# Modulation products of a diffusion layer queued on VectorE behind weight splits, and redistributed over the stages

## The chip, the cores and the metric

The kernel runs on one core of a Trainium2 chip. The metric is device time in microseconds, the median of three runs. Besides the three timed runs there is one execution with the hardware profiler, from which all rows below come.

## The reference, cut to what matters

One layer of a diffusion backbone in f32: 256 latent tokens and 256 context tokens, model width D = 2048, feed-forward width 5632. Six rows of modulation, each 2048 long, are computed from the condition vector and scale, shift and gate the two sub-layers:

```python
sh_m, sc_m, gt_m, sh_f, sc_f, gt_f = split(silu(c) @ w_ada + b_ada, 6)
h_lat = x * (1 + sc_m) + sh_m                 # the same for the context tokens
...                                           # h @ w_in: q, k, v, gates, decay; linear attention, pooling
mix = (gate_gla * y_gla + gate_pool * y_pool) @ w_out
x = layer_norm(ALPHA * x + gt_m * mix)
ffn = (silu(h2 @ w_gate) * (h2 @ w_up)) @ w_ffn_out      # h2 = x * (1 + sc_f) + sh_f
x = layer_norm(ALPHA * x + gt_f * ffn)
```

The first two rows of modulation (shift and scale of the mixer) are needed before anything else. The change is about how the other four, gt_m, sh_f, sc_f and gt_f, are computed: 4 x 2048 dot products of length 2048, done beside the rest of the layer.

## The kernel before

**Weights.** Every matrix arrives in units of 128 x 1024 f32 (512 KB). `weights` (L102) takes a unit: `raw_unit` issues its load on SP's queue (L95) into a ring of three buffers `raw`; `split` rounds it to a high part `hi` on ScalarE (L99) and forms the rest, `lo = raw - hi`, on VectorE (L100); TensorE multiplies both, `hi` with 512 columns (L128) and `lo` with 256 (L132) for stages where the weights stand still, or in three products (L158, L159, L161) where they move. A `raw` buffer is free, and the load of the unit three further on can be issued, when VectorE's subtraction has read it.

**Modulation products.** `ada(n)` (L252) does the next n units of 96: it loads 128 rows of the transposed modulation matrix on the same SP queue (L264, `w_adaT`) into a buffer `ra`, and VectorE multiplies them with the condition row and adds up each row (L265, a product with accumulator read; the result goes to one column of `mods`). `ra` is a ring too: of `NAK` = 3 buffers during keys and q, of one during gates and heads, of `NRA` = 2 during the merge. A load waits on SP for the product that last used its buffer, and everything behind it on SP waits with it.

`ada` is called at places that the tuple `ADA` counts: after each of the 16 key tiles (`ADA[2]` units), after each q tile (`ADA[1]`), after each gate block behind the first (`ADA[5]`), and after each column tile `ct` of the merge (`ADA[3]`, and all that is left from `ct` = 13 on). Entries 0 and 4 are for the values at the start, where no buffer for products exists yet. The last 32 units, gt_f, are done within the FFN, tiles 12 to 39, one a tile and two in every eighth (L874 to L876), in a ring of three inside the buffer `fa`.

**Order.** The program says what depends on what. A scheduler with a priority heap gives each engine its order; the splits of weights have raised priority (`high_priority(PW)`). `tc.issue_after(ins)` adds an edge: the instruction may stand in its engine's order only behind `ins`. Before, the products have no such edge, and the scheduler may place them as soon as their buffer and load allow.

**Stages** in the trace of before: values up to 239 us, keys to 335, first half of q to 358, gates, heads and pooling to 614, merge (16 column tiles of 7 weight units) to 944, the output projection w_o to 1048, the FFN's first matrices (44 tiles of 4 units, w_fi) to 1553, its last matrix to 1801. `rows(i)` (L749) loads the layer norm's gain and bias on POOL's queue, twice 1 MB; `rows(1)` takes the place of `fa` after the last product of the FFN. `add_mods` sums the finished columns, and `bcast_cols` (L727) spreads gt over the partitions for the residual (L755).

## Time and profile before

| | us |
|---|---|
| timed runs: lowest, median, highest | 1811.80, 1814.71, 1817.25 |
| profiled execution, its own time | 1810.72 |
| its span in the trace | 1808.9 |
| TensorE busy (PE) | 1754.6 |
| VectorE busy (DVE) | 1163.7 |
| ScalarE busy (ACT) | 804.3 |
| mean granted TensorE clock | 0.991 of full speed |

The profiled execution is 4.0 us faster than the median; 1.8 us of it lie outside the span. In rows of the trace each line gives a start and a duration in us, the engine, the line in the code, the operation and its tiles (`ps<-h,hi` reads "ps written from h and hi"), how many instructions the row joins (x8), and in brackets for how long the engine had been idle before it and what released it. PE's matmuls are pipelined, so that rows overlap a little. Windows show for each engine the busy time within the window.

### The profile page before, as it was taken

Reading aid. Unit: us, or ns where it says so; the run is one execution under the profiler, and the core shown is the slowest. Engines: PE = TensorE matmul, PEld = TensorE weight load, DVE = VectorE, ACT = ScalarE, POOL = GpSimd, SP = SyncE. Lnnn points to the kernel's source line nnn. Section 1 sums busy time; section 2 is a strip of 40 time slices with the busy share of each in tenths; the row PEclk is TensorE's granted clock in tenths of the full one; section 3 lists DMA queues with packets and bytes.
Section 4 is the critical chain, followed back from the end, with each engine's and each line's share of the span. In section 5 each row is a group of like instructions: output and inputs, shape, how many; then the busy total and the mean of one; then the engine's idle time right before and its main releaser. Section 6 shows DMA issues by size and latency. Waiting matters only on the chain.

```text
span 1808.9 us, 24699 instructions
## 1 busy us (share of the span) xinstructions
PE 1754.6 (97%) x9520; PEld 1469.2 (81%) x9520; DVE 1163.7 (64%) x1729; ACT 804.3 (44%) x1181; POOL 9.1 (1%) x19
## 2 busy tenths in 40 slices
PE   6999999999999999999999989999999999999996
PEld 4667888877777788888887878888878888888886
DVE  2555486587778788765556756677855556554555
ACT  2122222374776444454444454454444444433332
POOL 0000000000000000000000000000000000000000
PEclk9999999999999999999999989999999999999998
DMA  9796276666335798865566535579865555555553
GB/s 351 261 360 225 97 263 210 236 223 215 123 107 187 240 311 306 275 205 188 187 245 223 196 126 189 186 280 314 313 243 188 187 189 183 187 197 191 193 188 127
DMA packets 109637, 394.14 MB, mean 218 GB/s; under 512 B 12208, under 2 KB 12848, under 8 KB 109008
## 3 DMA queue, kind: packets, MB, share of 16 engines
q1 hardware_dynamic: 107712, 384.06, 62.3%
q0 software_dynamic: 1808, 8.52, 1.3%
q8 instruction: 74, 1.21, 0.3%
q14 instruction: 43, 0.35, 0.1%
HBM read 390.43 MB, written 2.10 MB: 217 GB/s over the span
## 4 chain that ended last, share of the span: by engine, by line
PE 80%; DMA 10%; DVE 6%; issue 2%; ACT 2%; SPq 0%; DVEq 0%; ACTq 0%
PE ps L128 28%; PE ps L132 14%; PE ps L158 11%; PE ps L159 10%; PE ps L161 10%; DMA ra<-in_w_adaT 5%; DVE lo L100 2%; PE ps L279 2%; DMA fa<-in_w_adaT 1%; DMA raw<-in_w_o 1%; ACT hi L99 1%; PE ps L504 1%; PE ps L547 1%; DMA raw<-in_w_fi 1%; DVE ra L265 1%
## 5 line engine op out<-in xcount | busy, mean ns | idle before, releaser
L100 DVE TENSOR_TENSOR lo<-raw,hi 128x1024 fp32r<-128x1024 f32 x510 | 622.2, 1223 | 391.5 <-ACT hi L99 384.1
L99 ACT ACTIVATE hi<-raw 128x1024 fp32r<-128x1024 f32 x510 | 539.0, 1059 | 643.0 <-PE ps L159 214.3
L128 PE MATMUL ps<-h,hi 128*128 128x512 f32 x1408 | 357.5, 396 | 4.5 <-ACT hi L99 3.7
L128 PEld LDWEIGHTS ps<-h,hi 128*128 128x128 f32 x1408 | 255.9, 191 | 51.4 <-ACT hi L99 4.1
L128 PE MATMUL ps<-hl,hi 128*128 128x512 f32 x768 | 211.1, 392 | 0.5 <-ACT hi L99 0.5
L132 PEld LDWEIGHTS ps<-h,lo 128*128 128x128 f32 x1408 | 193.1, 191 | 15.9 <-DVE lo L100 2.2
L132 PE MATMUL ps<-h,lo 128*128 128x256 f32 x1408 | 198.1, 283 | 0.4 <-DVE lo L100 0.4
L265 DVE SCALAR_TENSOR_TENSOR ra<-ra,silb 128x1024 f32<-128x1024 f32 x96 | 117.2, 1222 | 72.3 <-DMA ra<-in_w_adaT 71.6
L128 PEld LDWEIGHTS ps<-hl,hi 128*128 128x128 f32 x768 | 139.3, 189 | 25.9 <-ACT hi L99 0.7
L158 PE MATMUL ps<-hi,hl 128*128 128x512 f32 x320 | 128.9, 404 | 9.1 <-ACT hi L99 7.9
L158 PE MATMUL ps<-hi,hid 128*128 128x512 f32 (+1 forms) x372 | 134.9, 369 | 0.0
L159 PE MATMUL ps<-hi,hid 128*128 128x512 f32 (+1 forms) x372 | 134.0, 369 | 0.0
L159 PE MATMUL ps<-hi,hl 128*128 128x512 f32 x320 | 126.2, 396 | 0.0
L132 PE MATMUL ps<-hl,lo 128*128 128x256 f32 x768 | 120.5, 282 | 0.0
L132 PEld LDWEIGHTS ps<-hl,lo 128*128 128x128 f32 x768 | 111.7, 190 | 7.0 <-DVE lo L100 0.2
L161 PE MATMUL ps<-lo,hl 128*128 128x512 f32 x320 | 93.2, 392 | 0.0
L161 PE MATMUL ps<-lo,hid 128*128 128x512 f32 x372 | 90.6, 369 | 0.0
L330 DVE TENSOR_TENSOR v<-ps,v 128x512 f32<-128x512 f32 x80 | 50.6, 683 | 59.3 <-PE ps L161 59.3
L158 PEld LDWEIGHTS ps<-hi,hl 128*128 128x128 f32 x320 | 60.4, 189 | 28.4 <-ACT hi L99 8.7
L158 PEld LDWEIGHTS ps<-hi,hid 128*128 128x128 f32 x372 | 69.9, 188 | 12.2 <-DVE xt L759 0.2
L159 PEld LDWEIGHTS ps<-hi,hid 128*128 128x128 f32 x372 | 70.0, 188 | 11.9
L161 PEld LDWEIGHTS ps<-lo,hid 128*128 128x128 f32 x372 | 66.2, 188 | 11.8
(248 smaller groups left out, 2087.2 us busy)
## 6 DMA issues: line engine op xcount, KB each, us to landing
raw<-in_w_fi SPq DMA_DIRECT2D x176, 512.0 KB, 3.8
ra<-in_w_adaT SPq DMA_DIRECT2D x96, 512.0 KB, 4.6
raw<-in_w_fo SPq DMA_DIRECT2D x88, 512.0 KB, 4.3
rw<-in_w_sh_sc SPq DMA_DIRECT2D x64, 512.0 KB, 8.0
raw<-in_w_bg SPq DMA_DIRECT2D x64, 512.0 KB, 4.3
raw<-in_w_v SPq DMA_DIRECT2D x32, 512.0 KB, 5.6
raw<-in_w_g SPq DMA_DIRECT2D x32, 512.0 KB, 4.3
raw<-in_w_go SPq DMA_DIRECT2D x32, 512.0 KB, 4.3
```

Of the source, the lines that this page charges most:

```text
L99: S.activation(hi, full, AF.Copy)
L100: return V.tensor_tensor(lo, full, hi.bitcast(F32), op=ALU.subtract)
L128: PE.matmul(o, hi[:, j * P:(j + 1) * P], act(n + j), start=(n + j == 0), stop=(n + j == nk - 1), skip_group_check=True)
L132: PE.matmul(o[:, :T], lo[:, j * P:(j + 1) * P], act(n + j)[:, :T], start=False, stop=(n + j == nk - 1), skip_group_check=True)
L158: PE.matmul(o, ah, hi[:, a:b], start=(n + j == k0), stop=False)
L159: PE.matmul(o, al, hi[:, a:b], start=False, stop=False)
L161: PE.matmul(o, ah, lo[:, a:b], start=False, stop=(n + j == end))
L265: V.scalar_tensor_tensor(r, r, 1.0, silb[half], op0=ALU.mult, op1=ALU.mult, accum_out=mods[:, half, i:i + 1])
L279: PE.matmul(pr[32 * g:32 * g + 32, :256], sil[:, kt, :], r[:, 256 * g:256 * g + 256], start=(u == 0), stop=(u == KT // per - 1), skip_grou ...
L330: V.tensor_tensor(dst, src, dst, op=ALU.add)
L504: PE.matmul(ex[:, :n], la[:, s, t, c * P:(c + 1) * P], cw[:, :n], start=(s == 0), stop=(s == 1))
L547: PE.matmul(scc[:, t * T:(t + 1) * T], kst[:, c, t * P:(t + 1) * P], q4[:, c].rearrange("p t i -> p (t i)"), start=(c == 0 and t == 0), st ...
```

## The change

`ADA` becomes (0, 1, 4, 2, 8, 8): four products instead of two behind each key tile, eight instead of twelve behind each gate block, and the rest of the 96 in the merge is taken from `ct` = 14 on, not 13. Every product gets an edge behind a split: those of `ada` behind the split that was written last in the program (`last_split`), those of the FFN behind the split of `hid`, the tile's result (`lo_ins`). Loads have no edge of their own. The number of products and loads stays as it was. Line numbers after the change are one to four higher.

```diff
--- before.py
+++ after.py
@@ -38,7 +38,7 @@
 PRI = 300
 GROUPS = {0: 2, 2: 2, 4: 2, 6: 2, 8: 4, 12: 4}
 STEPS = {0: 2, 2: 3, 4: 4, 6: 4, 8: 2, 12: 0}
-ADA = (0, 1, 2, 2, 8, 12)
+ADA = (0, 1, 4, 2, 8, 8)
 
 
 S_CT = 0
@@ -81,6 +81,7 @@
         return tc.tile_pool(name=name, bufs=1, space=bass.MemoryType.PSUM, reuse_waits="tile")
 
     cnt = [0]
+    last_split = []
 
     def nm(s):
         cnt[0] += 1
@@ -97,7 +98,8 @@
 
     def split(full, hi, lo):
         S.activation(hi, full, AF.Copy)
-        return V.tensor_tensor(lo, full, hi.bitcast(F32), op=ALU.subtract)
+        last_split[:] = [V.tensor_tensor(lo, full, hi.bitcast(F32), op=ALU.subtract)]
+        return last_split[0]
 
     def weights(src):
         r = raw_unit(src)
@@ -262,8 +264,9 @@
                     silu_row(silb[half], half)
                 r = pool.tile([P, U], F32, tag="ra", bufs=ada_bufs[-1], name=nm("ra"))
                 nc.sync.dma_start(r, w_adaT[64 * half + i])
-                V.scalar_tensor_tensor(r, r, 1.0, silb[half], op0=ALU.mult, op1=ALU.mult,
-                                       accum_out=mods[:, half, i:i + 1])
+                with tc.issue_after(last_split[0].ins):
+                    V.scalar_tensor_tensor(r, r, 1.0, silb[half], op0=ALU.mult, op1=ALU.mult,
+                                           accum_out=mods[:, half, i:i + 1])
 
 
         def ada_chunk(ci):
@@ -705,7 +708,7 @@
             V.tensor_tensor(sg, sg, sp, op=ALU.add)
             m = mT[ct // 8][:, ct % 8]
             split(sg, m[:, 0, :], m[:, 1, :])
-            ada(ADA[3] if ct < 13 else 128)
+            ada(ADA[3] if ct < 14 else 128)
 
 
         add_mods(0, 3)
@@ -873,8 +876,9 @@
                 half, i = divmod(fu, 16)
                 r = fa[:, fu % 3, :]
                 nc.sync.dma_start(r, w_adaT[64 * half + 48 + i])
-                V.scalar_tensor_tensor(r, r, 1.0, silf[half], op0=ALU.mult, op1=ALU.mult,
-                                       accum_out=mods[:, half, 48 + i:49 + i])
+                with tc.issue_after(lo_ins.ins):
+                    V.scalar_tensor_tensor(r, r, 1.0, silf[half], op0=ALU.mult, op1=ALU.mult,
+                                           accum_out=mods[:, half, 48 + i:49 + i])
                 fu += 1
         if f == 41:
             add_mods(3, 4)
```

What the edges and counts move is seen in the order of the engines. First SP in the FFN, where the products begin: `raw<-in_w_fi` is a load of a weight unit, `fa<-in_w_adaT` one of a product. Before:

```order
L875 DMA fa<-in_w_adaT 128x1024 x2
L95 DMA raw_10246<-in_w_fi 128x1024
L875 DMA fa<-in_w_adaT 128x1024
L95 DMA raw_10276<-in_w_fi 128x1024
L95 DMA raw_10298<-in_w_fi 128x1024
L95 DMA raw_10325<-in_w_fi 128x1024
L875 DMA fa<-in_w_adaT 128x1024
L95 DMA raw_10347<-in_w_fi 128x1024
L875 DMA fa<-in_w_adaT 128x1024
L95 DMA raw_10377<-in_w_fi 128x1024
L875 DMA fa<-in_w_adaT 128x1024
```

and with the change:

```order
L878 DMA fa<-in_w_adaT 128x1024 x2
L96 DMA raw_10246<-in_w_fi 128x1024
L878 DMA fa<-in_w_adaT 128x1024
L96 DMA raw_10276<-in_w_fi 128x1024
L96 DMA raw_10298<-in_w_fi 128x1024
L96 DMA raw_10325<-in_w_fi 128x1024
L878 DMA fa<-in_w_adaT 128x1024 x2
L96 DMA raw_10347<-in_w_fi 128x1024
L96 DMA raw_10377<-in_w_fi 128x1024
L96 DMA raw_10399<-in_w_fi 128x1024
L96 DMA raw_10426<-in_w_fi 128x1024
L878 DMA fa<-in_w_adaT 128x1024
```

Before, product loads alternate with weight loads, so that all 32 go out among 41 weight loads; with the change one follows four weight loads (two in tiles 12, 20, 28 and 36), through tile 39.

The second place is VectorE in the merge, from the split of one column tile's result (`mT`) on. `ra,mods<-ra,silb` is a product, `lo<-raw,hi` the split of a weight unit, `yt` and `ys` are the tile's sums. Before:

```order
L100 TENSOR_TENSOR mT_5018<-yt_5332,mT_5018 128x256
L141 TENSOR_TENSOR yt_5513<-ps_5468,yt_5513 128x256
L265 SCALAR_TENSOR_TENSOR ra_6729,mods<-ra_6729,silb_4576 128x1024
L100 TENSOR_TENSOR lo_5592<-raw_5589,hi_5591 128x1024
L265 SCALAR_TENSOR_TENSOR ra_6732,mods<-ra_6732,silb_4576 128x1024
L100 TENSOR_TENSOR lo_5618<-raw_5615,hi_5617 128x1024
L141 TENSOR_TENSOR yt_5513<-ps_5518,yt_5513 128x256
L265 SCALAR_TENSOR_TENSOR ra_6910,mods<-ra_6910,silb_4576 128x1024
L100 TENSOR_TENSOR lo_5653<-raw_5650,hi_5652 128x1024
L100 TENSOR_TENSOR lo_5675<-raw_5672,hi_5674 128x1024
L141 TENSOR_TENSOR ys_5514<-ps_5566,ys_5514 128x256
L265 SCALAR_TENSOR_TENSOR ra_6913,mods<-ra_6913,silb_4576 128x1024
L701 TENSOR_TENSOR yt_5513<-ys_5514,yt_5513 128x256
```

and with the change:

```order
L101 TENSOR_TENSOR mT_5030<-yt_5344,mT_5030 128x256
L268 SCALAR_TENSOR_TENSOR ra_5474,mods<-ra_5474,silb_4183 128x1024
L268 SCALAR_TENSOR_TENSOR ra_5477,mods<-ra_5477,silb_4183 128x1024
L101 TENSOR_TENSOR lo_5582<-raw_5579,hi_5581 128x1024
L143 TENSOR_TENSOR yt_5525<-ps_5480,yt_5525 128x256
L101 TENSOR_TENSOR lo_5604<-raw_5601,hi_5603 128x1024
L101 TENSOR_TENSOR lo_5630<-raw_5627,hi_5629 128x1024
L143 TENSOR_TENSOR yt_5525<-ps_5530,yt_5525 128x256
L101 TENSOR_TENSOR lo_5665<-raw_5662,hi_5664 128x1024
L101 TENSOR_TENSOR lo_5687<-raw_5684,hi_5686 128x1024
L143 TENSOR_TENSOR ys_5526<-ps_5578,ys_5526 128x256
L704 TENSOR_TENSOR yt_5525<-ys_5526,yt_5525 128x256
```

Before, products lie between most splits, four to five a column tile, and are used up after some seven tiles; with the change two lie together behind the split of `mT`, in every tile up to the last but one.

The third place is VectorE between the first half of q and the first gate weights. The last split of a q weight is `lo_2743` before and `lo_2791` with the change, the first gate weight's is `lo_2970` and `lo_3018`. Before:

```order
L100 TENSOR_TENSOR lo_2721<-raw_2718,hi_2720 128x1024
L142 SCALAR_TENSOR_TENSOR qT<-ps_2617,qT 128x256
L265 SCALAR_TENSOR_TENSOR ra_3748,mods<-ra_3748,silb_1935 128x1024
L100 TENSOR_TENSOR lo_2743<-raw_2740,hi_2742 128x1024
L142 SCALAR_TENSOR_TENSOR qT<-ps_2667,qT 128x256
L265 SCALAR_TENSOR_TENSOR ra_3751,mods<-ra_3751,silb_1935 128x1024
L100 TENSOR_TENSOR lo_2970<-raw_2967,hi_2969 128x1024
L100 TENSOR_TENSOR lo_2988<-raw_2985,hi_2987 128x1024
L100 TENSOR_TENSOR lo_3006<-raw_3003,hi_3005 128x1024
```

and with the change:

```order
L101 TENSOR_TENSOR lo_2741<-raw_2738,hi_2740 128x1024
L268 SCALAR_TENSOR_TENSOR ra_2762,mods<-ra_2762,silb_1935 128x1024
L101 TENSOR_TENSOR lo_2769<-raw_2766,hi_2768 128x1024
L144 SCALAR_TENSOR_TENSOR qT<-ps_2665,qT 128x256
L101 TENSOR_TENSOR lo_2791<-raw_2788,hi_2790 128x1024
L268 SCALAR_TENSOR_TENSOR ra_2812,mods<-ra_2812,silb_1935 128x1024
L556 MEMSET PT_2833 128x256
L556 MEMSET PT_3378 128x256
L144 SCALAR_TENSOR_TENSOR qT<-ps_2715,qT 128x256
L101 TENSOR_TENSOR lo_3018<-raw_3015,hi_3017 128x1024
L473 SCALAR_TENSOR_TENSOR wd_2830<-wd_2830,sm,wr_2828 64x512
L101 TENSOR_TENSOR lo_3036<-raw_3033,hi_3035 128x1024
```

Before, a product stands directly ahead of the last q split and another ahead of the first gate split; with the change another weight's split lies between the product and the last q split, and the product behind it is the last one before the gate splits.

## Rows read from the trace of the kernel before

**Rows 1.** The page's first part: busy time of each engine, share of the span, instructions.

```profile
PE 1754.6 (97%) x9520; PEld 1469.2 (81%) x9520; DVE 1163.7 (64%) x1729; ACT 804.3 (44%) x1181; POOL 9.1 (1%) x19
```

**Rows 2.** The page's groups of instructions: the split on VectorE and the products; after the bar busy us and mean ns of one, then idle time ahead of them.

```profile
L100 DVE TENSOR_TENSOR lo<-raw,hi 128x1024 fp32r<-128x1024 f32 x510 | 622.2, 1223 | 391.5 <-ACT hi L99 384.1
...
L265 DVE SCALAR_TENSOR_TENSOR ra<-ra,silb 128x1024 f32<-128x1024 f32 x96 | 117.2, 1222 | 72.3 <-DMA ra<-in_w_adaT 71.6
```

**Rows 3.** The page's DMA issues: the loads for the products, with the median us from issue to landing.

```profile
ra<-in_w_adaT SPq DMA_DIRECT2D x96, 512.0 KB, 4.6
```

**Rows 4.** TensorE's timeline, FFN behind the last product: starts of two units, 16 units apart.

```profile
1346.64 2.00 PE L128 MATMUL ps<-h,hi 128*128 128x512 f32 x8
...
1391.34 2.00 PE L128 MATMUL ps<-h,hi 128*128 128x512 f32 x8
```

**Rows 5.** TensorE's timeline, FFN with the last products: the start of a unit, the longest wait and the half unit behind it, and the start of the unit 14 further on than the first.

```profile
1290.71 1.55 PE L128 MATMUL ps<-h,hi 128*128 128x512 f32 x6
...
1329.78 3.78 PE L128 MATMUL ps<-h,hi 128*128 128x512 f32 x8 [2.87 <-ACT hi L99]
1333.35 1.91 PE L132 MATMUL ps<-h,lo 128*128 128x256 f32 x8
...
1338.27 2.00 PE L128 MATMUL ps<-h,hi 128*128 128x512 f32 x8
```

**Rows 6.** Windows in the FFN: window, its us, busy us (x instructions) of PE, PEld, DVE, ACT and POOL, granted clock, DMA share, GB/s.

```profile
1250.00:1300.00 50.00, 50.00 (x288) 43.78 (x287) 40.01 (x59) 23.18 (x34) 0.00 (x0) 1.00 0.87 310
...
1320.00:1330.00 10.00, 7.13 (x42) 6.15 (x42) 3.70 (x9) 3.50 (x7) 0.18 (x1) 0.96 0.94 365
1330.00:1340.00 10.00, 10.00 (x40) 8.50 (x41) 7.27 (x10) 5.38 (x8) 0.00 (x0) 0.70 0.63 210
...
1350.00:1400.00 50.00, 50.00 (x289) 44.02 (x288) 28.68 (x37) 24.01 (x37) 0.00 (x0) 1.00 0.59 188
```

**Rows 7.** The chain of work that ended last, from 1270 to 1330 us: start, duration, what. Only its transfers are copied.

```profile
1274.96 4.92 DMA fa<-in_w_adaT
...
1307.39 7.32 DMA fa<-in_w_adaT
...
1320.08 8.48 DMA raw<-in_w_fi
```

**Rows 8.** POOL's timeline: the two issues of `rows`.

```profile
936.21 1.05 POOL L752 DMA_DIRECT2D rows<-in_lnrows  x2 [340.85 <-PE ps L132]
...
1319.13 1.05 POOL L752 DMA_DIRECT2D rows<-in_lnrows  x2 [127.67 <-DVE sg L856]
```

**Rows 9.** TensorE's timeline in the merge: the start of a unit, two waits, and the start of the unit 18 further on than the first.

```profile
694.92 2.00 PE L128 MATMUL ps<-hl,hi 128*128 128x512 f32 x8
...
706.04 1.21 PE L132 MATMUL ps<-y,lo 128*128 128x256 f32 x8 [0.36 <-DVE lo L100]
707.77 0.96 PE L128 MATMUL ps<-hl,hi 128*128 128x512 f32 x3 [0.52 <-ACT hi L99]
...
748.60 1.78 PE L128 MATMUL ps<-hl,hi 128*128 128x512 f32 x7
```

**Rows 10.** Windows in the keys, the end of the pooling stage, the merge, and the end of the merge with the start of w_o; columns as in rows 6.

```profile
240.00:270.00 30.00, 30.00 (x164) 26.08 (x163) 26.01 (x44) 5.11 (x8) 0.61 (x1) 1.00 0.91 313
...
600.00:640.00 40.00, 39.11 (x211) 33.88 (x212) 31.86 (x50) 20.98 (x34) 0.00 (x0) 1.00 0.80 264
...
660.00:680.00 20.00, 20.00 (x116) 17.58 (x115) 16.34 (x24) 9.19 (x14) 0.00 (x0) 1.00 0.94 328
...
900.00:950.00 50.00, 50.00 (x281) 43.73 (x280) 28.67 (x38) 22.80 (x33) 1.05 (x2) 1.00 0.69 242
```

**Rows 11.** Timelines of VectorE, SP's queue, ScalarE and TensorE between q and the gates.

```profile
347.48 1.23 DVE L100 TENSOR_TENSOR lo<-raw,hi 128x1024 fp32r<-128x1024 f32 x1 [0.57 <-ACT hi L99]
...
350.83 1.23 DVE L265 SCALAR_TENSOR_TENSOR ra<-ra,silb 128x1024 f32<-128x1024 f32 x1 [1.80 <-DMA ra<-in_w_adaT]
...
353.06 1.28 SPq L95 DMA_DIRECT2D raw<-in_w_g  x3
...
359.34 1.06 ACT L99 ACTIVATE hi<-raw 128x1024 fp32r<-128x1024 f32 x1 [5.41 <-DMA raw<-in_w_g]
...
360.45 0.50 PE L158 MATMUL ps<-hi,hl 128*128 128x512 f32 x1 [2.19 <-ACT hi L99]
...
368.12 0.39 PE L490 MATMUL ps<-cm,la 128*128 128x256 f32 x1 [2.14 <-ACT la L99]
```

**Rows 12.** Timelines of VectorE and TensorE at the end of the last head.

```profile
597.52 1.23 DVE L265 SCALAR_TENSOR_TENSOR ra<-ra,silb 128x1024 f32<-128x1024 f32 x1 [2.24 <-DMA ra<-in_w_adaT]
...
600.36 0.66 PE L590 MATMUL ps<-sm,o 128*128 128x128 f32 x4 [1.43 <-DVE o L588]
```

**Rows 13.** Timelines of VectorE and TensorE in the FFN without products: a split of a weight, and the matmuls that read it.

```profile
1511.84 1.23 DVE L100 TENSOR_TENSOR lo<-raw,hi 128x1024 fp32r<-128x1024 f32 x1 [1.23 <-ACT hi L99]
...
1518.88 1.11 PE L132 MATMUL ps<-h,lo 128*128 128x256 f32 x8
```

**Rows 14.** VectorE's timeline: the first product of the broadcast of gt_m.

```profile
954.22 0.68 DVE L736 TENSOR_TENSOR dg<-sm,fs 128x512 fp32r<-128x512 f32 x1
```

**Rows 15.** TensorE's timeline in the keys: starts of two units that follow each other.

```profile
296.54 0.40 PE L128 MATMUL ps<-hl,hi 128*128 128x512 f32 x1
...
302.11 0.40 PE L128 MATMUL ps<-hl,hi 128*128 128x512 f32 x1
```

## The prediction

> **What bounds the kernel now.** I read the share of each engine first, then the table of windows of 10 to 50 us, then the timelines of the windows in which TensorE was not busy throughout. TensorE is busy for 97% of the span [rows 1], so a gain can only come from stretches in which it stood still or ran at less than its full clock. In the change's territory there are four such stretches; the first step is to price each.
>
> The product that is moved costs VectorE 1222 ns, about as much as the split's second half, 1223 ns [rows 2], and it brings one 512 KB load that lands in about 4.6 us [rows 3]. A weight unit has the same size. So what the products do to TensorE is read as load on the DMA engines and as place in VectorE's queue.
>
> *FFN.* Where nothing disturbs it, unit follows unit in (1391.34 - 1346.64) / 16 = 2.794 us [rows 4]. Between the starts at 1290.71 and 1338.27 lie 14 units; they took 47.56 us and not 14 x 2.794 = 39.1, which is a **loss of 8.45 us** [rows 5]. It is one wait of 2.87 us for a weight's first half at 1329.78 with smaller ones before it, and then a stretch at half the pace: 3.57 us from one half unit to the next at 1333.35, where 1.84 is usual, the granted clock 0.70 in that window [rows 5, 6]. A mean of 0.70 says that the lower of the two levels (1.2 GHz) was granted for part of it; the engine had just been idle. What released that wait is a chain of loads, each waiting for a product and each product for its load, 4.9 to 7.3 us a link, with a weight's load of 8.48 us at its end [rows 7]. By the listing, all 32 product loads go out among 41 weight loads: 73 x 0.524 MB in 41 x 2.794 = 114.6 us would need 334 GB/s, while the window before the stall moves 310 (and one after the products 188) [rows 6]. At 310 the 73 loads take 123.5 us, 8.9 more, which is about the loss: for these ten tiles the kernel is bound by its loads, and the buffers put off the bill until 1329. At 1319.13, with the last product just over, the POOL queue sends two 1 MB rows into the same engines [rows 8].
>
> *Merge.* The same mechanism, weaker: 18 units from 694.92 to 748.60 took 53.68 us against 50.29, a **loss of 3.4 us**, in small waits as at 706.04 and 707.77 [rows 9], while the window before ran at 328 GB/s [rows 10].
>
> *From q to the gates.* VectorE's product at 350.83 waits 1.80 us for its own load; the second half of the last q weight stands behind it and ends at 353.2, about when SP may issue the first gate load (353.06), which reaches ScalarE at 359.34; TensorE stood **2.19 us** at 360.45 and 2.14 at 368.12 [rows 11].
>
> *Heads.* At 597.52 a product holds up the normalisation for 2.24 us of waiting, and TensorE loses **1.43 us** at 600.36 [rows 12].
>
> **The change part by part.** Nothing is added: 96 and 32 products, the same bytes. The edge behind the split is only an order on VectorE's own queue, so it costs no instruction; I take 0 for it.
>
> 1. *FFN products behind hid's split.* SP now has one product load for four weight loads in most tiles: 5 loads per 4 x 2.794 = 11.2 us, an estimate of 235 GB/s, up to 282 in the four tiles that have two, against 310 before the stall [rows 6]. No link of the chain of loads then follows directly on another, since each product lies a tile behind the last and its ring of three was refilled long ago. I take back the whole 8.45 us. Lower bound: the clock and the waits stay because the POOL rows still come, gain 0 (rival A). On VectorE the product fits into the idle time: it stood 1.23 us before the split at 1511.84, where no product lies [rows 13]. If it is late by a whole product (1.3 us with its accumulator read), the cover is the lead of that split: it ends at 1513.07 and its matmuls start at 1518.88, 5.8 us later [rows 13]. Two products in a row (2.6 us) stay under it too.
>
> 2. *Merge, two products per column tile.* 9 loads in 7 units, 9 x 0.524 MB / 19.6 us = 241 GB/s (estimate), where the four to five products a tile of before made it 295 to 321. Both follow the mT split, 2.6 us against the 5.8 of cover. Gain 3.4; bounds 0 and 3.4. The products now last into column tile 14, some 30 us before the end of this stage at about 944. Their sums go through the small modulation steps into the broadcast, whose first product before was at 954.22 [rows 14]; so about 40 us are left and I cost it at nothing. Without that cover, the w_o residual would wait for them.
>
> 3. *Keys, four products per tile.* Two weight loads and four product loads per tile. A key unit takes 302.11 - 296.54 = 5.57 us [rows 15], so 6 x 0.524 MB / 11.14 us = 282 GB/s (estimate). The trace has 313 GB/s in the first 30 us of the keys with TensorE busy for 30.00 of 30.00 us [rows 10]. Three products in a row are 3.9 us, behind a split of 1.2: 5.1 of 5.57 us. Cost 0; upper bound in rival B.
>
> 4. *q to the gates.* No product stands directly ahead of the last q split now, so the 1.80 us of waiting and the product's own 1.2 leave the path to the first gate load. One unit of 2.79 us behind the split before it (347.48), it would start at 350.3 and not, behind the product, at 352.0: 1.7 us earlier [rows 4, 11]; the first gate load then goes out alone and not as one of three, and 6.3 us of landing should come nearer to the 4.6 of a usual one [rows 3, 11]. Together that is more than TensorE's wait of 2.19, so it goes: gain 2.2. Bounds: 0, if what holds the load is the two loads of constants whose buffers the gate weights take, and 4.3, if the second wait goes too.
>
> 5. *Gates and heads.* 28 products with a ring of one. The wait at 597.52 may go (gain 1.4), but the listing puts products between other steps of a normalisation, each good for 1.3 us if it lands there without waiting. I set 0, with bounds +3 and -3: two such waits either way, by the nearest row, 1.43 [rows 12].
>
> Sum: -8.5 - 3.4 - 2.2 = -14.1 us. I round to 13.5, since the POOL rows, moved to a later place, may take a little there. On the profiled execution (1810.72 us, of which 1808.9 are span) that gives 1797.2. The median of the three runs is 1814.71, 4.0 above the profiled one; against it the forecast is **1801 us**. A difference of 0.3% (5.4 us) is about what a measurement of this kernel can tell from none.
>
> **The rivals.**
>
> *A. The FFN stall only moves.* rows(1) takes the buffer of the product loads, so its two 1 MB transfers follow the last product, then near 1319, now near the end of the FFN's tile 39. If they alone starve the weights, the 8.48 us load comes back there [rows 7]. For it: the stall sits exactly behind the issue at 1319.13 [rows 8]. Against it: the first rows(0) pair, issued at 936.21, met the w_o weights and eight x loads, and its window 900 to 950 has TensorE busy for 50.00 of 50.00 us [rows 8, 10]; and small waits precede 1319 already, with weights' buffers empty from the products. It would leave 8.45 us in place: 14.1 - 8.45 = 5.6 less than before, 1809.1. The page "DMA: Bandwidth & Descriptors" of the Trainium skill, section "Queues, rings and completion order", has each DMA engine take turns between the queues it serves, a packet at a time; by that rule the POOL rows would take about half of the engines as long as they last, wherever they are issued. The trace agrees only so far: the weight's load doubles at 1320.08 but nothing stalls after 936.21 [rows 6, 7, 10].
>
> *B. The keys become bound by their loads.* The rate needed is 282 GB/s; the stretch 600 to 640, also split between a ring of products and weights, moved only 264 [rows 10]. At 264 a tile takes 6 x 0.524 / 264 = 11.9 us, 0.8 more, over eight tiles 6 us. Time 1801 + 6 = 1807. Against it: 313 in the keys themselves.
>
> *C. Slower: products hold the path in gates and heads.* With a ring of one, a load starts only after the product before it, and lands 4.6 us later [rows 3]. Where two products lie close together, on either side of a decay step or a normalisation that TensorE waits for, the second holds that step up to 4.6 us. Before, such a wait of 2.24 us cost TensorE 1.43 at the one place shown [rows 12]. It decides from three such places on: 3 x 4.6 = 13.8 us eats the gains of the other parts. Priced at one in four of the 28 products that the listing leaves to q's second half and the heads, 7 x 4.6 = 32 us, the time is 1801 + 32 = 1833. For it: VectorE takes its queue in order, and a split behind such a product waits too. Against it: VectorE is busy for 64% only [rows 1], and the program places 12 products fewer there (24 after the gate blocks, not 36).
>
> *D. It does not do what it says on the chip.* SP and VectorE take their queues in order, but a product that had to wait before may still be the one that waits: the loads bunch again behind the x, row and gate loads, and the stalls return at other places, with no change, 1811 to 1817. Against it: the listing has the loads one by one among the weights.
>
> **How the numbers follow.** My forecast, gains in FFN and merge without a new loss: 0.58. A: 0.14. B: 0.08. C: 0.10. D: 0.10. Faster by over 0.3% (under 1809.3) takes in the forecast, B, and two thirds of A's cases, which lie about 1809 where the whole stall comes back and lower where part of it does: 0.58 + 0.08 + 0.09 = 0.75. Within 0.3%: the rest of A, D and a little of C, 0.05 + 0.10 + 0.02 = 0.17. Slower: 0.08. For the range the best case is 1814.7 - 8.45 - 3.4 - 4.3 - 3 = 1795.6, with the 2 us that medians of three differ by 1793.5; at the upper end it reaches over A, B and a part of D to 1813. That leaves out C (0.10), the upper part of D and the little below.
>
> **What the profile of the changed kernel would show.** Step 1: the FFN's windows all with 288 or 289 matmuls in 50 us and a clock of 1.00, no wait of ScalarE over 2 us for w_fi, and product loads at even distances. Step 2: no wait of TensorE in the merge windows, with about 240 GB/s up to the last column tiles. Step 3: still no gap in the keys, at some 280 GB/s. Step 4: no wait at the first gate matmul. Step 5: waits of VectorE for w_adaT smaller in sum. The prediction is wrong if a stall of several us follows the POOL rows near the end of the FFN (A), if TensorE waits in the keys (B), or if the gates show more TensorE waits behind a product (C).

## The result and the profile after

The changed kernel takes 1800.24 us, the median of six runs, against 1813.32 for the kernel before beside it: a ratio of 0.9934, 95% interval 0.9917 to 0.9951, or 13.1 us. The forecast was 1801 us. Its profiled execution takes 1799.62 us with a span of 1797.8, which is 11.1 us shorter than the span of before.

Where those 11.1 us lie is read from TensorE's timeline: a stage lasts from the first matmul of its kind to the first of the next. The same table serves the experiments below (us; "gates to merge" holds gates, heads, pooling and merge, which overlap).

| execution | values | keys, first half of q | gates to merge | w_o | FFN, first matrices |
|---|---|---|---|---|---|
| before | 221.86 | 121.23 | 583.68 | 104.34 | 504.42 |
| changed | 222.12 | 119.05 | 584.53 | 104.29 | 494.96 |
| e1_ffn_edge | 222.93 | 122.34 | 584.90 | 108.66 | 494.89 |
| e2_ada_edge | 224.96 | 119.50 | 611.86 | 109.21 | 505.29 |
| e3_counts | 222.80 | 128.30 | 582.93 | 104.91 | 506.21 |
| e4_no_ffn_edge | 222.98 | 119.15 | 584.01 | 106.96 | 506.70 |
| e5_rows_late | 225.93 | 121.62 | 583.35 | 106.83 | 504.81 |
| e12_rows_wait | 223.06 | 121.94 | 587.85 | 106.63 | 501.47 |
| e6_cross_late | 222.90 | 119.02 | 594.23 | 113.35 | 494.83 |
| e7_one_row | 223.42 | 119.01 | 578.52 | 107.19 | 496.79 |
| e8_after_again | 223.40 | 119.03 | 584.12 | 108.91 | 495.47 |
| e9_own_tmp | 224.86 | 119.35 | 582.75 | 107.13 | 495.23 |
| e10_own_tmp_late | 221.98 | 119.49 | 585.08 | 106.63 | 495.57 |
| e11_heads_free | 223.40 | 119.35 | 582.94 | 106.94 | 495.33 |

So the FFN gives 9.46 us and the edge to the gates 2.18; from gates to merge, where 3.4 were expected, 0.85 is lost; the rest, with 0.54 at the very start, is noise. The w_o stage, in code that no kernel here touches, varies from 104 to 109 us between executions (113.35 in e6, whose last products reach into it): smaller differences than that are read from a stage, not from a total.

Two of these columns join several things. In the FFN, what the change aimed at lies between the first matmul of tile 13 and that of tile 25 (tiles counted from 0). First before, where tile 25 starts at 1338.27 [rows 5], with a window at the start of the FFN, then changed:

```profile
1195.74 1.09 PE L128 MATMUL ps<-h,hi 128*128 128x512 f32 x4
...
1048.00:1053.00 5.00, 4.53 (x13) 3.66 (x14) 2.39 (x6) 2.46 (x7) 0.00 (x0) 0.54 0.00 0
```

```profile
1192.24 1.09 PE L130 MATMUL ps<-h,hi 128*128 128x512 f32 x4
...
1326.32 0.86 PE L130 MATMUL ps<-h,hi 128*128 128x512 f32 x3
...
365.18 0.39 PE L493 MATMUL ps<-cm,la 128*128 128x256 f32 x1 [0.45 <-ACT la L100]
```

These twelve tiles took 142.53 us and take 134.08 now, 8.45 less. The first tile of the FFN is 1.84 us shorter, which the change did not do: TensorE waits 5.11 us at the end of w_o in both kernels, and before, the lower clock behind that wait reached into the FFN (0.54 in its first 5 us, 1.00 in the changed kernel). The last three tiles take 0.82 us more, 36.68 against 35.86; they take 0.7 to 1.3 more in every execution with the FFN's edges.

From gates to merge, the second wait of rows 11, 2.14 us at 368.12, is down to 0.45 (the last row above), which gives 1.7; the last 1728 matmuls ahead of w_o take 301.68 us and not 305.11, which gives 3.4. As the column lost 0.85 all the same, 6.0 us were lost in between, in the heads. The three executions of the changed kernel's code up to there (changed, e8 and e4) lie within 0.5 us of each other, the four of the old code (before, e1, e5 and e12) between 583.35 and 587.85.

The windows of the changed kernel in the keys, the merge, the FFN where the stall was [rows 6], and its last tiles (columns as in rows 6):

```profile
240.00:335.00 95.00, 95.00 (x540) 83.59 (x538) 62.54 (x97) 24.03 (x34) 0.72 (x1) 1.00 0.76 263
...
640.00:760.00 120.00, 120.00 (x689) 105.60 (x688) 85.27 (x120) 58.82 (x88) 0.00 (x0) 1.00 0.71 239
1300.00:1350.00 50.00, 50.00 (x288) 44.04 (x287) 32.27 (x44) 24.28 (x36) 0.00 (x0) 1.00 0.73 239
1500.00:1550.00 50.00, 49.27 (x268) 42.36 (x267) 31.36 (x44) 25.75 (x39) 1.05 (x2) 1.00 0.61 219
```

and the merge window of before:

```profile
640.00:760.00 120.00, 118.24 (x670) 102.55 (x669) 100.56 (x158) 55.65 (x82) 0.00 (x0) 1.00 0.88 303
```

TensorE is busy throughout in the keys, the merge and the FFN's window at full clock; only near the FFN's end is a little missing. In the merge it runs 689 matmuls instead of 670 in 120 us, at 239 GB/s instead of 303; 19 matmuls at 0.174 us are 3.3 us, as the 3.4 above. The products themselves, on the page, beside the lines of rows 1 and 2:

```profile
PE 1751.0 (97%) x9520; PEld 1469.6 (82%) x9520; DVE 1165.7 (65%) x1729; ACT 802.4 (45%) x1181; POOL 9.1 (1%) x19
...
L268 DVE SCALAR_TENSOR_TENSOR ra<-ra,silb 128x1024 f32<-128x1024 f32 x96 | 114.9, 1221 | 9.8 <-DMA ra<-in_w_adaT 9.5
```

They cost as much as before (1221 ns), but VectorE's idle time ahead of them fell from 72.3 to 9.8 us. Between q and the gates (answering to rows 11: SP's queue, ScalarE, TensorE):

```profile
350.80 0.33 SPq L96 DMA_DIRECT2D raw<-in_w_g  x1
...
357.01 1.06 ACT L100 ACTIVATE hi<-raw 128x1024 fp32r<-128x1024 f32 x1 [0.94 <-DMA raw<-in_w_g]
...
357.99 0.40 PE L160 MATMUL ps<-hi,hl 128*128 128x512 f32 x1
```

The first gate load leaves 2.3 us earlier, reaches ScalarE as long after its issue as before (6.2 us), and TensorE does not wait. In the heads there is a wait that no row of before has. ScalarE, SP's queue, POOL and TensorE:

```profile
482.60 0.58 POOL L194 DMA_DIRECT2D silb<-in_c_row  x1 [13.50 <-DVE ra L268]
...
482.75 13.69 SPq L96 DMA_DIRECT2D raw<-in_w_g  x3
...
488.46 1.06 ACT L180 ACTIVATE raw<-silb 128x1024 f32<-128x1024 f32 x1 [4.28 <-DMA silb<-in_c_row]
489.43 0.58 ACT L508 ACTIVATE bun<-ps 128x512 f32<-128x512 f32 x1
...
492.80 0.80 PE L536 MATMUL ps<-bun 128*128 128x128 f32 x2 [2.53 <-DVE bun L526]
```

and the windows around it:

```profile
490.00:495.00 5.00, 2.20 (x7) 1.44 (x6) 3.76 (x15) 5.00 (x12) 0.00 (x0) 0.75 0.02 3
495.00:500.00 5.00, 5.00 (x22) 4.14 (x21) 3.42 (x4) 1.76 (x2) 0.00 (x0) 0.50 0.31 105
500.00:505.00 5.00, 5.00 (x12) 3.02 (x12) 3.66 (x6) 1.71 (x3) 0.00 (x0) 0.72 0.60 202
```

The products of the second half of the 96 need the second condition row (`silb`, of c_ctx). It has one buffer, so POOL fetches it when the 48th product is done, and ScalarE takes its silu in `silu_row`, with a buffer of the weights' ring for work space. With the new counts (32 products in the eight key tiles, 4 and 4 with the q tiles) the 48th is the last of the eight behind the second gate block; before it was the last of the twelve behind the third. ScalarE now stands 4.28 us for the row, ahead of the exponentials of the decay; of the three weight loads in SP's row the third leaves 11 us after the second (at 496.11 and 484.72); TensorE loses 2.53 us and then runs at the lower level of its clock until about 503.

Before, the row was fetched at 438.27 and ScalarE read it, without a wait, at 527.30. The two `rows` loads on POOL, and ScalarE's longest wait for a weight behind the second:

```profile
934.60 1.05 POOL L755 DMA_DIRECT2D rows<-in_lnrows  x2 [333.99 <-PE ps L134]
...
1500.36 1.05 POOL L755 DMA_DIRECT2D rows<-in_lnrows  x2 [312.40 <-ACT sg L141]
...
1510.55 1.06 ACT L100 ACTIVATE hi<-raw 128x1024 fp32r<-128x1024 f32 x1 [4.83 <-DMA raw<-in_w_fi]
```

Behind 1500.36 TensorE has one wait, 0.73 us at 1519.69 for the broadcast of gt_f, which has nothing to do with a weight. But a weight was late there for ScalarE: the load issued at 1501.20 was read at 1510.55, after a wait of 4.83 us. That is almost the 5.09 us that ScalarE waited at 1328.67 in the old stall:

```profile
1328.67 1.06 ACT L99 ACTIVATE hi<-raw 128x1024 fp32r<-128x1024 f32 x1 [5.09 <-DMA raw<-in_w_fi]
```

There TensorE stood 2.87 us behind it [rows 5], here not at all. With waits of 3.60 us at 1209.42 and 3.25 at 1240.92, one sign of step 1, no wait of ScalarE over 2 us for w_fi, did not come.

### The profile page after: what moved, and what is told of

Its sections match the earlier page's. It is cut to its first block, busy times and chain, and to the rows that moved or that the text cites. A ratio compares the mean times of both kernels' runs of the same rounds, so it can differ in the third digit from the quotient of the medians.

```text
span 1797.8 us, 24697 instructions
## 1 busy us (share of the span) xinstructions
PE 1751.0 (97%) x9520; PEld 1469.6 (82%) x9520; DVE 1165.7 (65%) x1729; ACT 802.4 (45%) x1181; POOL 9.1 (1%) x19
## 4 chain that ended last, share of the span: by engine, by line
PE 64%; DMA 3%; DVE 3%; ACT 2%; issue 1%; ACTq 0%; DVEq 0%
PE ps L130 29%; PE ps L134 15%; PE ps L160 6%; PE ps L161 5%; PE ps L163 5%; DMA raw<-in_w_o 1%; DMA raw<-in_w_fi 1%; ACT hi L100 1%; DVE lo L101 1%; PE ps L578 1%; PE ps L550 1%; DMA raw<-in_w_p 0%; PE ps L659 0%; DMA silb<-in_c_row 0%; DVE xt L904 0%
## 5 line engine op out<-in xcount | busy, mean ns | idle before, releaser
L130 PE MATMUL ps<-h,hi 128*128 128x512 f32 x1408 | 353.4, 392 | 1.0 <-DVE h L101 1.0
L268 DVE SCALAR_TENSOR_TENSOR ra<-ra,silb 128x1024 f32<-128x1024 f32 x96 | 114.9, 1221 | 9.8 <-DMA ra<-in_w_adaT 9.5
```

Source lines behind the costliest of these rows:

```text
L130: PE.matmul(o, hi[:, j * P:(j + 1) * P], act(n + j), start=(n + j == 0), stop=(n + j == nk - 1), skip_group_check=True)
L268: V.scalar_tensor_tensor(r, r, 1.0, silb[half], op0=ALU.mult, op1=ALU.mult, accum_out=mods[:, half, i:i + 1])
```

## The experiments

The theory was the prediction's: bunched product loads empty the weights' ring. Its rivals were the rows on POOL's queue and the counts alone.

**e1_ffn_edge: only the FFN's edges, on the kernel before.**

```diff
+                with tc.issue_after(lo_ins.ins):
-                V.scalar_tensor_tensor(r, r, 1.0, silf[half], ...
+                    V.scalar_tensor_tensor(r, r, 1.0, silf[half], ...
```

> The kernel before with one part of the change alone: the 32 products of the FFN stand behind the split of hid; the 96 others and their counts as before. Theory 1 (the FFN's stall comes from product loads bunched among 41 weight loads): the whole stall goes, the FFN's 504.4 us become 495, the kernel is 8.5 to 9.5 us faster than before, ratio about 0.995, and everything ahead of the FFN stays within 1 us. Theory 2 (the two 1 MB rows on POOL's queue starve the weights wherever they fall): a stall of 2 us or more follows the rows at about 1510 us and the gain is under 4 us. Theory 3 (the gain lies in the counts, more products in the keys): no change, ratio 1.000.

1807.81 us, ratio 0.9955 (0.9940 to 0.9971), an interval that overlaps the whole change's. The FFN takes 494.89, as in the changed kernel, and the window that held the stall is full:

```profile
1300.00:1350.00 50.00, 50.00 (x289) 44.03 (x288) 32.67 (x45) 24.12 (x36) 0.00 (x0) 1.00 0.73 247
```

**e4_no_ffn_edge: the changed kernel without the FFN's edges** (the same diff the other way).

> The changed kernel without the edges in the FFN. Theory 1: the FFN's stall is back at about the same place with rows(1) behind it: 8.5 to 9.5 us slower than the changed kernel, 1809 to 1810, ratio to before 0.998; all ahead of the FFN as in the changed kernel, with the wait of about 2.5 us in the heads. Theory 2 and 3: within 2 us of the changed kernel (2: the stall there is due to the rows, whichever place they have; 3: the gain lies in the counts), ratio 0.993 to 0.995.

1816.88 us, ratio to before 1.0009 (0.9994 to 1.0024): without this part nothing measurable is left of the gain. By the ratios it is 13.6 us behind the changed kernel, more than the 8.5 to 9.5 expected; of the profiled executions' difference 2.7 us lie in w_o and 2.1 in the FFN's first tile. It also says that the edges and counts of the 96 have no gain that the total shows: most of what they win in keys, gates and merge is lost in the heads. The FFN is back at 506.70, with the wait in its old place:

```profile
1334.78 1.65 PE L130 MATMUL ps<-h,hi 128*128 128x512 f32 x3 [2.77 <-ACT hi L100]
```

**e3_counts: only the counts**, no edge.

```diff
-ADA = (0, 1, 2, 2, 8, 12)
+ADA = (0, 1, 4, 2, 8, 8)
...
-            ada(ADA[3] if ct < 13 else 128)
+            ada(ADA[3] if ct < 14 else 128)
```

> The kernel before with the counts alone (four products a key tile, eight a gate block, the rest from column tile 14 on); no edge anywhere. Theory 1: the scheduler still places products as early as their buffers allow, so they bunch in the keys (three loads between two weights) and in the merge; FFN unchanged, merge stall about as before, 1811 to 1815, ratio 1.000. Theory 3: the counts carry the gain, 1802 to 1806, ratio 0.994 to 0.997.

1822.52 us, ratio 1.0040 (1.0025 to 1.0056): slower, where I had no change. Without an edge the scheduler sets the products ahead of weight splits and of the evacuation of a finished key tile. VectorE and TensorE:

```profile
278.10 1.23 DVE L265 SCALAR_TENSOR_TENSOR ra<-ra,silb 128x1024 f32<-128x1024 f32 x1 [1.78 <-DMA ra<-in_w_adaT]
...
279.34 1.22 DVE L265 SCALAR_TENSOR_TENSOR ra<-ra,silb 128x1024 f32<-128x1024 f32 x1
...
281.62 0.42 DVE L141 TENSOR_TENSOR kT<-ps,kT 128x256 f32<-128x256 f32 x1
...
282.10 0.49 PE L128 MATMUL ps<-hl,hi 128*128 128x512 f32 x1 [1.28 <-DVE kT L141]
```

Keys and q lose 7 us (128.30 against 121.23). Four products a tile are free in the keys only behind their edge.

**e2_ada_edge: only the edges of the 96**, old counts.

```diff
+                with tc.issue_after(last_split[0].ins):
-                V.scalar_tensor_tensor(r, r, 1.0, silb[half], ...
+                    V.scalar_tensor_tensor(r, r, 1.0, silb[half], ...
```

> The kernel before with the edges of the 96 ada products alone; counts as before, no edge in the FFN. Theory 1: the FFN keeps its stall of some 8.5 us; the merge loses its small waits (gain 3.4) and the first gate matmul its wait of 2.2; the second condition row is now fetched behind the 48th product within the heads, where it costs about as much as in the changed kernel, 4 to 6 us, so that keys to merge together gain 0 to 3 us and the ratio is 0.998 to 1.001. Theory 3 (the counts carry the gain): no change in any stage, ratio 1.000. If the edges were harmless in the heads: 5.5 us faster, ratio 0.997.

1846.99 us, ratio 1.0176 (1.0159 to 1.0193). This is far outside what I expected. Keys and q gain their 1.7 us; gates to merge lose 28. SP's queue, and VectorE and TensorE:

```profile
526.33 49.50 SPq L266 DMA_DIRECT2D ra<-in_w_adaT  x10
575.92 21.27 SPq L96 DMA_DIRECT2D raw<-in_w_p  x6
...
542.59 1.23 DVE L268 SCALAR_TENSOR_TENSOR ra<-ra,silb 128x1024 f32<-128x1024 f32 x1 [1.93 <-DMA ra<-in_w_adaT]
...
586.63 0.80 PE L160 MATMUL ps<-hi,hl 128*128 128x512 f32 x1 [5.09 <-ACT hi L100]
```

Ten product loads in a row, in a ring of one, hold SP for 49.5 us, each behind the product ahead of it, and the weights of the pooling stage stand behind them. It is the prediction's rival C, with SP's queue as its place rather than VectorE's. So the edges and counts of the 96 need each other: either alone makes the kernel slower.

**e5_rows_late and e12_rows_wait: the kernel before, with rows(1) late.** In the first, an edge behind the last hid split; in the second, whose lines follow, a write that the loads must wait for:

```diff
+        if f == 42:
+            with tc.issue_after(lo_ins.ins):
+                V.memset(fa[:, 0, 0:1], 0.0)
```

> The kernel before with one edge more: the two 1 MB loads of rows(1) on POOL's queue are issued behind the last hid split (about 1550 us), not behind the last product (1319); the products stay bunched. Theory 1 (bunched product loads empty the weights' ring): the FFN keeps waits of TensorE near 1315 to 1330; the part of the loss that remains is what the bunch costs alone, 4 to 8.5 us of 8.45, ratio 0.998 to 1.000. Theory 2 (the rows do it): the wait of 2.87 us and the low clock vanish, the FFN takes at most 497 us, ratio about 0.996. Both together would show as about half the loss, with waits below 1 us and no clock drop.

> The kernel before, in which a one-column memset of the product loads' buffer behind the hid split of tile 42 now holds back rows(1): in e5_rows_late the edge did not delay it, it was issued at 1327 all the same, right behind the last product. Here its two 1 MB transfers should be issued near 1545 us. Products bunched as before. Theory 1 (the bunched product loads empty the weights' ring): TensorE still waits near 1315 to 1330, and at least half of the FFN's 8.45 us of loss stays; ratio 0.9975 to 1.000. Theory 2 (the rows do it): no wait of 2 us and no clock below 1.00 near 1330, the FFN takes at most 497 us, ratio about 0.995. Both together (the product loads use up the lead, the rows then cost the weight that has none): the long wait goes and waits under 1 us stay, the FFN takes 496 to 499 us.

The first tells nothing on the rows: POOL issued them at 1327.37, right behind the last product; the edge, to a split on VectorE, did not hold back POOL. Its ratio is 0.9998 (0.9986 to 1.0010), and the wait of 2.70 us is there at 1337.85. In the second they go out at 1552, and these are POOL's row, the windows of the old stall, and one wait of TensorE:

```profile
1552.06 1.05 POOL L752 DMA_DIRECT2D rows<-in_lnrows  x2 [354.46 <-DVE fa L881]
...
1320.00:1330.00 10.00, 9.32 (x51) 7.67 (x51) 7.01 (x13) 3.85 (x6) 0.00 (x0) 1.00 0.79 275
1330.00:1340.00 10.00, 10.00 (x58) 8.55 (x57) 7.92 (x13) 5.83 (x10) 0.00 (x0) 1.00 0.68 218
...
1328.12 1.22 PE L132 MATMUL ps<-h,lo 128*128 128x256 f32 x8 [0.35 <-DVE lo L100]
```

The long wait and the clock drop of rows 5 and 6 are gone; waits of 0.2 to 0.5 us from 1227 to 1328 stay. The FFN takes 501.47 us, 3.0 less than before, but 1.8 of that are the first tile at full clock. The tiles 13 to 24 take 141.43 us, 7.35 more than in the changed kernel: so much do the bunched products cost without the rows. With the rows at their old place the same tiles lost 8.45 us before and 10.68 in e5, 9.05, 12.07 and 10.44 in e2, e3 and e4. So the bunch makes most of the loss, and the rows behind it add 1 to 5 us, which one execution can't size better; the ratio, 0.9987 (0.9967 to 1.0006), can't tell that from none. At 934.60 and 1500.36 in the changed kernel, where no bunch of product loads went ahead, TensorE waited for no weight.

**e7_one_row: the changed kernel with the first row in place of the second.**

```diff
+                if half and 0 in silb:
+                    silb[1] = silb[0]
                 if half not in silb:
```

> The changed kernel, which leaves out the second condition row: its load and its silu are not done and the second half of the products uses the first row. Theory 4: ScalarE's wait of 4.28 us for that row goes, TensorE's gap of 2.53 us near 493 and the clock of 0.50 to 0.75 behind it vanish; gates plus merge take 578 to 580 us, not 584.5; 4 to 6 us faster than the changed kernel, ratio 0.990. Rival 5 (products themselves cost the heads): under 1.5 us faster, ratio 0.993.

It leaves out the second row, so half of its products are of the wrong row. 1799.13 us, ratio 0.9919 (0.9907 to 0.9932). Gates to merge take 578.52, 6.0 less than in the changed kernel, with no wait near 493 and a full clock:

```profile
490.00:495.00 5.00, 5.00 (x24) 3.98 (x24) 4.45 (x12) 3.48 (x9) 0.00 (x0) 1.00 0.83 270
495.00:500.00 5.00, 5.00 (x32) 4.14 (x31) 4.51 (x12) 1.06 (x1) 0.00 (x0) 1.00 0.50 170
```

So the row costs 6 us in that stage, of which 2.53 are TensorE's wait; the rest, the lower clock and what follows, was not measured apart. The 6.0 are all that the heads lost above. The total shows less of it, since FFN and w_o took 4.7 us more in this execution.

**e6_cross_late: the changed kernel with the 48th product moved into the merge.**

```diff
-ADA = (0, 1, 4, 2, 8, 8)
+ADA = (0, 1, 4, 3, 8, 2)
```

> The changed kernel with other counts: two products behind each gate block instead of eight and three behind each column tile of the merge instead of two, so that 46 are done when the heads end and the second condition row is fetched in the merge, not in the heads. Theory 4 (the row's load and its silu on ScalarE, placed between the decay steps, make the heads' new wait of 2.5 us and the clock drop behind it): the heads lose that wait, the merge stays without gaps at some 268 GB/s, 4 to 6 us faster than the changed kernel, 1794 to 1796, ratio 0.990. Rival 5 (the products in the heads' queue themselves cost it): also faster, by 1 to 3 us, with waits of VectorE gone rather than of ScalarE. Rival 6 (the row costs the same wherever it falls): same as the changed kernel, with a gap of 2 us or more early in the merge.

1824.90 us, ratio 1.0058 (1.0044 to 1.0072). The heads lose their wait, as expected, but the kernel is slower, not 4 to 6 us faster: the row costs more where it falls now. SP, POOL, ScalarE and TensorE:

```profile
647.62 15.91 SPq L96 DMA_DIRECT2D raw<-in_w_bg  x4
...
647.47 0.53 POOL L194 DMA_DIRECT2D silb<-in_c_row  x1 [52.23 <-DVE ra L268]
...
654.04 1.06 ACT L180 ACTIVATE raw<-silb 128x1024 f32<-128x1024 f32 x1 [9.62 <-DMA silb<-in_c_row]
655.12 1.28 ACT L181 ACT_TABLE_LOAD   x1
...
658.47 2.93 PE L130 MATMUL ps<-hl,hi 128*128 128x512 f32 x6 [16.28 <-ACT hi L100]
```

ScalarE waits 9.62 us for the row with the weights' splits behind it, loads its tables for the silu, and TensorE stands for 16.28 us. Products also last into w_o here. So moving the row's load is not enough; the place where the row is read has to be one without a wait.

**e8 to e11: the changed kernel again, and three ways around the row**, on one chip. The first is the kernel itself. In e9 the silu has a buffer of its own; in e10 it also stands behind the head's last exponential; in e11 the 24 products behind the gate blocks have no edge.

```diff
 # e9; in e10 the line with silu(z, z, ...) stands under tc.issue_after(last_e[0].ins)
-                    silu_row(silb[half], half)
+                    if half:
+                        nc.gpsimd.dma_start(silb[half], c_row[half].partition_broadcast(P))
+                        for j in range(2):
+                            z = silb[half][:, 512 * j:512 * j + 512]
+                            silu(z, z, pool.tile([P, 512], F32, tag="silt", name=nm("silt")))
+                    else:
+                        silu_row(silb[half], half)
 # e11, with ada's new argument left out
-                ada(ADA[5])
+                ada(ADA[5], edge=False)
```

> The changed kernel itself once more, beside the three that follow, on their chip. Every theory: ratio 0.992 to 0.995 to the kernel before; gates plus merge 583 to 586 us, with the wait of about 2.5 us near 493 and the lower clock behind it.

> The changed kernel with a work buffer of its own (two halves of 512 columns) for the silu of the second condition row, where the changed kernel takes one of the three buffers of the weights' ring. Theory 7 (the cost in the heads comes from the ring: while the row is on its way, the next weight loads wait on SP for the buffer that the silu holds): no stretch of 13 us in which SP has three weight loads waiting, TensorE's wait near 493 under 1 us, gates plus merge 579 to 581, 3 to 5 us faster than the changed kernel beside it. Theory 4 in its narrow form (ScalarE's wait for the row ahead of the exponentials does it): the wait of 2 to 4 us on ScalarE stays and so does TensorE's; within 1.5 us of the changed kernel.

> As the kernel ahead of it, with the silu queued behind the last exponential of that head's decay, so that ScalarE never waits for the row. Theory 4 (narrow): ScalarE's wait and TensorE's near 493 go, gates plus merge 578 to 581, 4 to 6 us faster than the changed kernel beside it, unless the products that now come later crowd the end of the heads and the pooling, where each load that SP takes ahead of a weight can cost up to 4.6 us. Theory 7: as e9_own_tmp, within 1.5 us of it.

> The changed kernel without the edge for the 24 products behind the gate blocks; the 72 others and the FFN's keep theirs. If the edge is what costs in the heads: gates plus merge 579 to 582, 3 to 5 us faster than the changed kernel beside it. If the edge does nothing there and the counts decide (24 products instead of 36 behind the gate blocks): within 2 us of the changed kernel.

| | median us | ratio to before | 95% interval |
|---|---|---|---|
| e8_after_again | 1806.60 | 0.9946 | 0.9928 to 0.9965 |
| e9_own_tmp | 1801.35 | 0.9922 | 0.9894 to 0.9950 |
| e10_own_tmp_late | 1805.40 | 0.9934 | 0.9910 to 0.9958 |
| e11_heads_free | 1804.66 | 0.9935 | 0.9909 to 0.9961 |

e8 repeats the result. In e9 and e10, ScalarE's and SP's rows, then e10's window and a later wait of TensorE:

```profile
491.96 0.63 ACT L180 ACTIVATE silt<-silb 128x512 f32<-128x512 f32 x1 [1.67 <-DMA silb<-in_c_row]
...
488.68 12.11 SPq L96 DMA_DIRECT2D raw<-in_w_g  x4
```

```profile
495.00:500.00 5.00, 5.00 (x17) 3.10 (x17) 0.72 (x2) 0.87 (x2) 0.00 (x0) 1.00 0.32 105
...
554.79 10.58 SPq L274 DMA_DIRECT2D ra<-in_w_adaT  x3
...
578.25 0.80 PE L161 MATMUL ps<-hi,hl 128*128 128x512 f32 x1 [2.85 <-ACT p L244]
```

e9 shortens ScalarE's wait to 1.67 us, TensorE's to 1.47, and keeps the clock full there; a wait of 1.85 us at 604.02, which the changed kernel does not have, and a lower clock behind it take some of that back. Its median is 5 us under the changed kernel's, but the intervals overlap, and gates to merge show only 1.4 us; it is the fastest whole layer here, by a margin that isn't settled. Neither theory came out whole. Theory 4 (narrow) wanted ScalarE's wait to stay. Of theory 7, 579 to 581 us did not come, but the time without a weight load on SP fell from 11 us to 8 (from 492.17 to 500.46; before, 492.28 to 500.15 at the same place). How much of the 6 us is the ring's and how much ScalarE's wait stays open. e10 takes the wait near 493 away altogether, and gives it back: the products come later, TensorE waits 1.94 us at 550, and, behind three product loads that hold SP for 10.58 us, 2.85 at 578.

e11 lies within 2 us, but what it loses lies elsewhere. POOL, ScalarE and TensorE:

```profile
467.54 0.55 POOL L194 DMA_DIRECT2D silb<-in_c_row  x1 [70.24 <-DVE ra L268]
...
480.38 1.05 ACT L180 ACTIVATE raw<-silb 128x1024 f32<-128x1024 f32 x1
...
579.46 0.50 PE L160 MATMUL ps<-hi,hl 128*128 128x512 f32 x1 [3.24 <-ACT p L243]
```

Without the edge the 48th product runs 15 us earlier, ScalarE finds the row there, and the wait near 493 is gone; another of 3.24 us, in the pooling stage, takes its place. Over the kernels:

| | row fetched | read by ScalarE | its wait for the row |
|---|---|---|---|
| before | 438.27 | 527.30 | none |
| e3, counts alone | 381.60 | 490.79 | none |
| e11, changed without the heads' edge | 467.54 | 480.38 | none |
| changed | 482.60 | 488.46 | 4.28 |
| e2, edges alone | 575.77 | 581.24 | 3.10 |

As far as these five show, the counts set where ScalarE reads the row, and the edge holds back the 48th product, and with it the fetch, until shortly before that place.

## Why the prediction was right

**Step 1, FFN: right.** 8.45 us forecast, 8.45 measured in the tiles of the old stall; the 9.46 of the whole stage hold a first tile that was 1.84 shorter by chance and last tiles that are 0.82 longer. I had argued that bunched loads alone explain all of it (8.9 us of excess); alone they make 7.35 (e12); what went beyond that, 1 to 5 us over five executions, came with the rows. The clock stays at 1.00 through the old stall. The 0.6 us that I took off in rounding, for the rows at their later place, stand against those 0.82.

**Step 2, merge: right.** 3.4 forecast, 3.4 measured in the last 1728 matmuls. The sums of the products were in time for the broadcast: the last product started at 935.06, the broadcast's first at 951.96.

**Step 3, keys: right,** at no cost, 263 GB/s against the estimate of 282. There are eight key tiles, as rival B counts them, not 16. That this hangs on the edge, as e3 shows, I had not seen; rival B did not occur.

**Step 4, q to the gates: right at the first gate matmul, 2.18 for 2.2, partly wrong in the reason.** The load left 2.3 us earlier, but landed no faster (6.2 us). The second wait of rows 11 fell by 1.7 us as well, so the gain is 3.9, near the upper bound of 4.3.

**Step 5, gates and heads: this failed.** I set 0 within 3; the heads lost 6.0 us. The loss is not products between steps of a normalisation, where I looked. The step that failed is the sentence that nothing is added and only places move: the 48th product moved, and with it the row's load and silu, which I had not listed among the things that move. Taken away, the row is worth 6.0 us in that stage (e7), the whole loss. I had also taken 0 for the edge itself: without it behind the gate blocks ScalarE does not wait for the row (e11), though the stage as a whole is little shorter.

**The sum: near, and partly by luck.** The parts of the change add up to 8.45 + 3.43 + 2.18 + 1.69 - 6.0 = 9.8 us, less 0.8 at the FFN's end. The profiled executions differ by 11.1, not 13.5; the FFN's first tile (1.84) and the start (0.54) are in it, and neither is the change's. That the medians differ by 13.1 is within what they move by: for the kernel before, three runs gave 1814.71 and six 1813.32, and e8 repeats the comparison with 10.5. So a loss of 6.0 that I did not see was covered by the second gate wait, by chance, and by the width of the measurement.

**Rivals.** A was partly right, as a part of the old stall, and wrong as a forecast: at their later place the rows cost at most what the last tiles lost, 0.8 us here, where the broadcast now falls too. C did not occur here but is real: e2 shows it at 28 us. I gave it 0.10; it was the new counts that kept it away. The page "DMA: Bandwidth & Descriptors" of the Trainium skill (section "Queues, rings and completion order") says that the engines take turns between queues. The trace agrees at both places: ScalarE waited 5.09 us for a weight behind the rows of before and 4.83 behind those of the changed kernel. But sharing alone made TensorE wait for no weight at 1500.

## What to carry to other kernels

Side work that streams its own operands should be placed by rate: compare its loads and the main stream's with what the windows show was carried without a wait, and spread it to stay below. Tie it to the main work on the engine that consumes it, and count it so that a stretch with a shallow ring gets little: order and count are one decision, and for the 96 products each half alone lost 0.4 to 1.8% here. Measure the parts too: the FFN's edge alone gave a ratio of 0.9955, the edges and counts of the 96 alone 1.0009. When counts change, look for what hangs on the n-th item (a refill, a table, a buffer that changes hands), and cost that too.

## What the runs showed of the hardware

A TensorE wait of 2.87 us in the old FFN stall and one of 2.53 in the heads were followed by windows at 0.50 to 0.75 of the clock, for some 10 us in the heads; the waits up to 0.5 us in e12 were followed by none. The same wait in e4 (the heads at 495.71), 2.73 us, was followed by none either:

```profile
495.71 0.49 PE L536 MATMUL ps<-bun 128*128 128x128 f32 x2 [2.73 <-DVE bun L526]
...
490.00:510.00 20.00, 16.69 (x71) 10.91 (x70) 13.97 (x30) 12.91 (x26) 0.00 (x0) 1.00 0.48 168
```

So waits of this length may or may not cost clock as well, and a stage can differ by it between executions, as the FFN's first tile does (1.84 us). Not expected, too: behind a 2 MB load from another queue ScalarE waited some 5 us for a weight in both kernels, but TensorE stood only where a bunch of product loads had gone ahead.
